# Expert weights in two-way float32r halves, or in raw float32 for groups of 64 and 32 slots: a mixture-of-experts stage on one core

## The chip, the core and the metric

One NeuronCore of a Trainium2 chip runs the whole kernel, one launch for one sequence. The metric is device time in microseconds (us), lower is better. The engines are TensorE (PE), VectorE (DVE), ScalarE (ACT), GpSimd (POOL) and SyncE (SP); SP's queue issues the weight loads.

## The reference

A decoder trunk of two layers on x, 1 x 256 x 1024, all in float32. Each layer has a token mixer and then a channel mixer; both are scaled and shifted by a conditioning vector, and added to x through a gate vector. Layer 0's channel mixer is one dense SwiGLU, layer 1's is this:

```python
logits = h @ router_w                                   # 256 tokens x 8 experts
top_v, top_i = lax.top_k(logits, 2)
gates = jnp.sum(one_hot(top_i, 8) * softmax(top_v)[..., None], axis=-2)
y = jnp.zeros_like(h)
for e in range(8):
    y = y + gates[..., e:e + 1] * ((silu(h @ w1[e]) * (h @ w3[e])) @ w2[e])
x = x + gt_f * y                                        # and a last RMSNorm
```

Here w1 and w3 are 1024 x 2816 and w2 is 2816 x 1024 for each expert. Of all weights, only those of the experts are 277 MB. Each token goes to two of the eight experts.

## The kernel before, in words

The kernel computes both layers up to the router as a *front* that lasts to about 476 us, and then the *expert stage*, which the function `experts` (L761) writes.

**Places.** The experts stand in eight *places*: expert 0 in place 0, the others in places 1 to 7 in descending order of how many tokens chose them (`place`, L861). Each place has a fixed number of *slots* (token rows): 128 in the three *wide* places 0 to 2, 64 in the four places 3 to 6, 32 in place 7 (`slots`, L921). A token past the last slot is taken up by a second pass at the end (L1233 on) that runs only if a flag says so.

**Weights.** Every place streams 33 pieces of 1 MiB (128 x 2048 float32): eleven each of w1, w3 and w2. `load` (L132) issues one DMA on SP's queue, in program order, into the next free tile that `slot` (L122) hands out: in the expert stage first a list `once` (L776: 3 tiles of pool `ahead`, 4 of `more`, 6 of `rawp`, then tiles named `xn` and `big`), and after that `more` and `rawp` in turn, 10 tiles (L779). The 264 loads are all of this form; SP takes them in order, and a load whose tile is not free holds those behind it.

**A wide place.** `prepare` (L928) gathers the place's tokens by matmuls with one-hot matrices (L973), and leaves them as a high and a low float32r part, `x_hi` and `x_lo`. `inner` (L1056) makes six *chunks* of the hidden layer, five of 512 columns and one of 256. Each weight piece is split by `split` (L137) into two halves of 1024 columns, each again a high part (ACT, L145) and a low part (DVE, L146), and `mm3` (L156) issues three float32r matmuls for each product, high by high, high by low and low by high (L157 to L159), on the full 128 x 128 array:

```python
pe.matmul(ps, l_hi, r_hi, ...)      # L157
pe.matmul(ps, l_hi, r_lo, ...)      # L158
pe.matmul(ps, l_lo, r_hi, ...)      # L159
```

`turn` (L996) transposes the chunk. `outer` (L1094) multiplies by w2 in eleven *units*, one weight piece each, again through `split` and `mm3`. `scatter` adds the result to the tokens' rows by matmuls with one-hot matrices.

**A narrow place** (3 to 7). No weight is split. `inner_narrow` (L1029) keeps the tokens in float32, `x_n`, and puts the 64 slots of w1's product into columns 0 to 63 of the array and those of w3's into columns 64 to 127; with 32 slots, each of those halves is halved again for even and odd k:

```python
r = H * i + m * (k % js)            # L1049: m slots, js = 64 // m
pe.matmul(ps[r:r + m, :n], x_n[:, k, :], w[:, kk * n:(kk + 1) * n], ...)
```

`outer` does the same with w2's two column halves (L1099), and `scatter` uses the two halves of the array's rows (L1155).

In the trace a float32 matmul stands as two rows with the form `128*64` (64 columns of the array) or `128*32`; a float32r one is one row, `128*128`.

**Order of the work.** Two streams run in turn: places 0 to 2 and places 3 to 7, each nine steps a place (six chunks, then the outer units in three steps of four, four and three). `TURNS` (L41) is a string of 0 and 1 that says which stream gives the next step. The tile framework sets each engine's queue by priorities within that. The PSUM banks: two of `pb` (wide outer results), two of `pm` (gathers, transposes, scatter), three of `pa` (inner chunks) and one of `po` (narrow outer results).

Of the kernel before, what the change touches and what calls it, by code (L numbers as in the profile page):

```python
# [8 lines left out]
F32 = mybir.dt.float32  # L9
# [19 lines left out]
MORE = 4  # L29
AHEAD = 3  # L30
# [7 lines left out]
HOLD_E = (0, 2, 1, 1, 1)  # L38
WIDE = 3
Q = 32  # L40
# [21 lines left out]
def trunk(  # L62
# [698 lines left out]
    def experts():  # L761
# [70 lines left out]
        def turned(oh, dt):  # L832

            tp = pm()
            tv = tp[:, :SEQ].rearrange("p (t s) -> p t s", t=NT)
            for t in range(NT):
                transpose(tv[:, t, :], oh[:, t, :].bitcast(F32))
            o = et([P, NT, P], "oht", dt, bufs=4)
            act.activation(o[:], tv, AF.Copy)
            return o  # L840

# [6 lines left out]
        pool.memset(cap[:, :WIDE], float(P))  # L848
        pool.memset(cap[:, WIDE:NE - 1], float(H))
        pool.memset(cap[:, NE - 1:], float(Q))  # L850
# [70 lines left out]
        def slots(p):  # L921
            return P if wide_place(p) else H if p < NE - 1 else Q

        def gate_of(p, t):
            return (gates[:, t, 0:1] if p == 0 else placed["gates"][t][:, p:p + 1])

        xe = {}
        def prepare(places):  # L928


            oh = et([P, NT, 2, P], "oh", F32R)
            at = {}
            for i, p in enumerate(places):
                n = slots(p)
                lo_ = i * P + (0 if i else P - n)
                at[p] = lo_, lo_ + n
                for t in range(NT):
                    slot_of = pos[:, t, 0:1] if p == 0 else placed["pos"][t][:, p:p + 1]
                    if wide_place(p):
                        ohi = dve.tensor_scalar(oh[:, t, i, :], iota[:], slot_of, None, op0=ALU.is_equal)  # L940
                    else:
                        ohi = dve.tensor_scalar(oh[:, t, i, :].rearrange("p (i s) -> p i s", s=n),
                                                iota[:, :n].unsqueeze(1).to_broadcast([P, P // n, n]), slot_of, None,
                                                op0=ALU.is_equal)
            base, end = at[places[0]][0], at[places[-1]][1]
            n = end - base
            marks = []
# [13 lines left out]
            xs_of = {}  # L961
            for p in places:
                if wide_place(p):
                    xs_of[p] = et([P, KD, P], "x_hi", F32R), et([P, KD, P], "x_lo", F32R)
                else:
                    xs_of[p] = et([P, KD, slots(p)], "x_n", bufs=2), None
            for k in range(0, KD, 2):
                gp = pm()
                gv = gp[:, :2 * n].rearrange("p (k s) -> p k s", k=2)
                for kk in range(2):  # L970
                    for i, src in enumerate((t_hi, t_lo)):
                        for t in range(NT):
                            pe.matmul(gv[:, kk, :], src[:, t, (k + kk) * P:(k + kk + 1) * P],  # L973
                                      oh[:, t].rearrange("p i s -> p (i s)")[:, base:end],
                                      start=(i + t == 0), stop=(i + t == NT))
                for p in places:
                    r = slice(at[p][0] - base, at[p][1] - base)
                    x_hi, x_lo = xs_of[p]
                    dst = et([P, 2, P], "h32", bufs=2)[:] if wide_place(p) else x_hi[:, k:k + 2, :]
                    for kk in range(2):  # L980
                        ai = act.activation(dst[:, kk, :], gv[:, kk, r], AF.Identity,
                                            bias=B[:, k + kk:k + kk + 1], scale=A[:, k + kk:k + kk + 1])
                    if not wide_place(p):
                        continue
                    dve.tensor_copy(x_hi[:, k:k + 2, :], dst)
                    di = dve.tensor_tensor(x_lo[:, k:k + 2, :], dst, x_hi[:, k:k + 2, :].bitcast(F32),  # L986
                                           op=ALU.subtract)
                    marks.append((ai, di))
            if places[0] == 0:
                hold((HOLD_E[0],), (HOLD_E[1], expd, ohi), *((n_, *m) for n_, m in zip(HOLD_E[2:], marks)))  # L990
            for i, p in enumerate(places):
                xe[p] = (*xs_of[p], turned(oh[:, :, i, :], F32R))

        aa = {}

        def turn(p, c, a):  # L996
# [3 lines left out]
            tp = pm()  # L1000
            tv = tp[:].rearrange("p (b s) -> p b s", b=4)
            for b in range(n):
                ti = transpose(tv[:, b, :], a[:, b * P:(b + 1) * P])
            o = slice(4 * c, 4 * c + n)
            if not aa:

                first.close()
                ap_ = ctx.enter_context(tc.tile_pool(name="inner", bufs=1, side="right", reuse_waits="tile"))
                aa["pool"] = ap_
            if c == 0 and wide_place(p):  # L1010
                for h in ("a_hi", "a_lo"):
                    aa[h] = aa["pool"].tile([P, KF, P], F32R, tag=h, name=nm(h))
            if not wide_place(p):
                m = slots(p)
# [382 lines left out]
```

## Time and profile before

| what | value |
|---|---|
| time, median of 3 runs | 1168.54 us (1166.7 to 1168.91) |
| the profiled execution's own time | 1168.7 us |
| span of its trace, first to last instruction | 1166.9 us |
| PE busy | 1107.4 us, 95% |
| DVE busy | 627.4 us, 54% |
| ACT busy | 518.3 us, 44% |
| moved by DMA | 395.69 MB, mean 339 GB/s |
| mean granted clock of TensorE | 0.979 |

The times of the runs are of the whole execution; the span is of the one profiled execution, and the rows and lines that are read from the trace count from its start. The trace lies 1.8 us below that execution's own time. An engine's busy share is an average over front and expert stage, which have different limits, so each stage has to be read by itself. A row that says `x8` merges eight instructions; its length is from the first one's start to the last one's end.

### The profile page before, as it was taken

To read this page: it belongs to the slowest core of one execution; us is meant where nothing else is said; L and a number is where in the kernel's file an instruction comes from. 1 tells how busy PE (TensorE), PEld (TensorE's weight loads), DVE (VectorE), ACT (ScalarE), POOL (GpSimd) and SP (SyncE) were. 2 spreads that over 40 slices of the span, in tenths; PEclk is the share of its full clock that TensorE was granted. 3 is DMA by queue.
4 is the path that set the end of the run, shared out by engine and by line. 5 is a ranking of instruction groups with operands and counts; after the bars stand their busy time and mean duration, and the time that the engine had idled before them with its cause. 6 is when DMAs were issued, how large, how long until landed. Compare 5 with 4: busy or idle time off the path is not lost.

```text
span 1166.9 us, 15801 instructions
## 1 busy us (share of the span) xinstructions
PE 1107.4 (95%) x6125; PEld 742.8 (64%) x6125; DVE 627.4 (54%) x818; ACT 518.3 (44%) x724; POOL 30.5 (3%) x69
## 2 busy tenths in 40 slices
PE   4899999999999999899999999999999999998993
PEld 2578779999777888686465445554455544655540
DVE  2668556757776765797135443353343633345442
ACT  2764444444437744786234333542342333434331
POOL 2000000000001000300000000000000000000000
PEclk9899999999999999899999999999999999998996
DMA  9977486858886447495999999999999999999994
GB/s 361 410 288 291 145 324 249 310 201 306 334 332 229 147 143 288 181 359 189 418 420 419 420 419 420 419 420 420 388 406 419 420 419 419 419 419 403 398 420 172
DMA packets 57182, 395.69 MB, mean 339 GB/s; under 512 B 8294, under 2 KB 8710, under 8 KB 9356
## 3 DMA queue, kind: packets, MB, share of 16 engines
q1 hardware_dynamic: 54272, 393.24, 84.2%
q10 hardware_dynamic: 2828, 1.37, 0.4%
q8 instruction: 50, 0.82, 0.3%
q14 instruction: 32, 0.26, 0.1%
HBM read 393.53 MB, written 1.05 MB: 338 GB/s over the span
## 4 chain that ended last, share of the span: by engine, by line
PE 88%; DMA 4%; ACT 3%; DVE 2%; POOL 1%; issue 1%; ACTq 0%; POOLq 0%; DVEq 0%; SPq 0%
PE pa L1050 17%; PE pa L158 8%; PE pa L157 8%; PE pa L159 8%; PE po L1099 7%; PE pa L406 6%; PE pa L407 6%; PE pa L408 6%; PE pb L158 4%; PE pb L159 4%; PE pb L157 4%; PE pm L226 2%; PE pb L261 2%; PE pm L973 2%; DMA bdx<-in_wx_dram 2%; ACT whi L145 2%
## 5 line engine op out<-in xcount | busy, mean ns | idle before, releaser
L146 DVE TENSOR_TENSOR wlo<-raw,whi 128x1024 fp32r<-128x1024 f32 x318 | 378.6, 1222 | 205.1 <-ACT whi L145 204.4
L145 ACT ACTIVATE whi<-raw 128x1024 fp32r<-128x1024 f32 x318 | 324.5, 1057 | 214.7 <-PE pa L407 90.2
L1050 PE MATMUL pa<-raw,x_n 128*64 128x512 f32 (+3 forms) x960 | 205.0, 562 | 0.0
L406 PE MATMUL pa<-wide_hi,whi 128*128 128x256 f32 x544 | 154.3, 284 | 0.2 <-DVE wide_hi L380 0.2
L407 PE MATMUL pa<-wide_lo,whi 128*128 128x256 f32 x544 | 153.5, 282 | 0.2 <-DVE wide_lo L381 0.2
L408 PE MATMUL pa<-wide_hi,wlo 128*128 128x256 f32 x544 | 153.5, 282 | 0.0
L1050 PEld LDWEIGHTS pa<-raw,x_n 128*64 128x64 f32 (+1 forms) x960 | 63.0, 131 | 106.7 <-issue 101.3
L158 PE MATMUL pa<-wlo,x_hi 128*128 128x512 f32 (+1 forms) x288 | 113.3, 394 | 3.7 <-DVE wlo L146 3.7
L157 PE MATMUL pa<-whi,x_hi 128*128 128x512 f32 (+1 forms) x288 | 110.7, 389 | 0.9 <-ACT whi L145 0.3
L159 PE MATMUL pa<-whi,x_lo 128*128 128x512 f32 (+1 forms) x288 | 109.9, 382 | 0.1
L406 PEld LDWEIGHTS pa<-wide_hi,whi 128*128 128x128 f32 x544 | 102.3, 188 | 6.4 <-issue 4.0
L407 PEld LDWEIGHTS pa<-wide_lo,whi 128*128 128x128 f32 x544 | 102.5, 189 | 1.6 <-issue 1.1
L408 PEld LDWEIGHTS pa<-wide_hi,wlo 128*128 128x128 f32 x544 | 102.5, 188 | 0.3 <-issue 0.3
L1099 PE MATMUL po<-raw,big 128*64 128x512 f32 (+1 forms) x440 | 93.4, 616 | 6.3 <-DMA raw<-in_m_dram 6.3
L1053 ACT ACTIVATE s<-pa 128x512 f32<-128x512 f32 (+1 forms) x30 | 16.9, 562 | 163.4 <-PE pa L1050 163.4
L158 PE MATMUL pb<-wlo,a_hi 128*128 128x512 f32 x176 | 71.6, 408 | 2.0 <-DVE wlo L146 2.0
L158 PEld LDWEIGHTS pa<-wlo,x_hi 128*128 128x128 f32 x288 | 55.3, 192 | 26.5 <-DVE wlo L146 6.7
L159 PE MATMUL pb<-whi,a_lo 128*128 128x512 f32 x176 | 69.8, 398 | 0.0
L157 PEld LDWEIGHTS pa<-whi,x_hi 128*128 128x128 f32 x288 | 55.3, 192 | 21.8 <-issue 7.7
L157 PE MATMUL pb<-whi,a_hi 128*128 128x512 f32 x176 | 60.8, 403 | 2.0 <-ACT whi L145 2.0
L1099 PEld LDWEIGHTS po<-raw,big 128*64 128x64 f32 (+1 forms) x440 | 25.4, 132 | 57.8 <-issue 49.8
L159 PEld LDWEIGHTS pa<-whi,x_lo 128*128 128x128 f32 x288 | 55.5, 193 | 10.0 <-DVE x_lo L986 0.8
(323 smaller groups left out, 1242.4 us busy)
## 6 DMA issues: line engine op xcount, KB each, us to landing
raw<-in_m_dram SPq DMA_DIRECT2D x263, 1024.0 KB, 10.6
raw<-in_ada_w_dram SPq DMA_DIRECT2D x48, 1024.0 KB, 7.3
raw<-in_f_dram SPq DMA_DIRECT2D x33, 1024.0 KB, 6.0
raw<-in_win_dram SPq DMA_DIRECT2D x20, 1024.0 KB, 6.3
raw<-in_wout_dram SPq DMA_DIRECT2D x8, 1024.0 KB, 6.1
xs<-in_x_dram SPq DMA_DIRECT2D x1, 1024.0 KB
big<-in_m_dram SPq DMA_DIRECT2D x1, 1024.0 KB
out_dram<-big SPq DMA_DIRECT2D x2, 512.0 KB, 3.2
```

The lines of the kernel that those rows point to most:

```text
L145: act.activation(hi[:, :n], src, AF.Copy)
L146: dve.tensor_tensor(lo[:, :n], src, hi[:, :n].bitcast(F32), op=ALU.subtract)
L157: pe.matmul(ps, l_hi, r_hi, start=first, stop=False)
L158: pe.matmul(ps, l_hi, r_lo, start=False, stop=False)
L159: return pe.matmul(ps, l_lo, r_hi, start=False, stop=last)
L226: return pe.transpose(o, i, ident[:i.shape[0], :i.shape[0]])
L261: pe.matmul(ps[o:o + 32, :], cact[:, k, :], wi[:, h * 512:(h + 1) * 512], start=(j == 0), stop=(j == 3))
L406: pe.matmul(pv[:, b, :], wh, h_hi[:, k, :], start=(k == 0), stop=False)
L407: pe.matmul(pv[:, b, :], wh, h_lo[:, k, :], start=False, stop=False)
L408: pe.matmul(pv[:, b, :], wl, h_hi[:, k, :], start=False, stop=(k == KD - 1))
L1050: pe.matmul(ps[r:r + m, :n], x_n[:, k, :], w[:, kk * n:(kk + 1) * n], start=(k < js), stop=(k >= KD - js))
L1099: pe.matmul(acc[r:r + m, :], aa["a_n"][:, k, :], w[:, i * 1024 + c * 512:i * 1024 + (c + 1) * 512], start=(k < js), stop=(k >= KF - js))
```

## The change

No weight of an expert is split any more. Each place is cut into *groups* of 64 or 32 slots (`GROUPS`): places 0 and 2 become 64 + 32 slots, place 1 becomes 64 + 64, places 3 to 7 keep one group. So places 0 and 2 have 96 slots in place of 128. `inner` and `outer` run every group of a place over the same raw float32 weight piece, in the form that the narrow places had. Tokens of wide places stay in float32 (`x_w`), the hidden layer too (`a_w`); the pool of split tiles now ends with the front, and `more` has 10 tiles in place of 4, `ahead` 2 in place of 3. Each group has its own bank and its own one-hot matrix for the scatter, made in a new function `spread` after the eighth unit. The second pass becomes a function that steps through the tokens past the slots 128 at a time.

```diff
-MORE = 4
-AHEAD = 3
+MORE = 10
+AHEAD = 2
...
+GROUPS = ((64, 32), (64, 64), (64, 32), (64,), (64,), (64,), (64,), (32,))
+SLOTS = tuple(sum(g) for g in GROUPS)
...
-    splp = ctx.enter_context(tc.tile_pool(name="splp", bufs=SPLIT_BUFS))
     front = ctx.enter_context(ExitStack())
+    splp = front.enter_context(tc.tile_pool(name="splp", bufs=SPLIT_BUFS))
...
             for p in places:
-                if wide_place(p):
-                    xs_of[p] = et([P, KD, P], "x_hi", F32R), et([P, KD, P], "x_lo", F32R)
-                else:
-                    xs_of[p] = et([P, KD, slots(p)], "x_n", bufs=2), None
+                xe[p] = (et([P, KD, SLOTS[p]], "x_w") if wide_place(p) else et([P, KD, SLOTS[p]], "x_n", bufs=2))
...
+        def groups(p):
+            lo = 0
+            for m in GROUPS[p]:
+                yield lo, m, H // m
+                lo += m
...
+        def spread(p):
+            aa["oht", p] = []
+            for lo, m, _ in groups(p):
+                oh = et([P, NT, P], "oh", F32R)
+                for t in range(NT):
+                    one_hot(oh[:, t, :].rearrange("p (i s) -> p i s", s=m), p, t, lo, m)
+                aa["oht", p].append(turned(oh, F32R))
...
-        def inner(e, c):
-            if not wide_place(e):
-                return inner_narrow(e, c)
...
-                            hi, lo = split(w[:, j * 1024:(j + 1) * 1024])
-                            for kk in range(2):
-                                k = 4 * h + 2 * j + kk
-                                mm3(ps[:], x_hi[:, k, :], x_lo[:, k, :], hi[:, kk * 512:(kk + 1) * 512],
-                                    lo[:, kk * 512:(kk + 1) * 512], k == 0, k == KD - 1)
...
+        def inner(p, c):
+            pss = [pa() for _ in GROUPS[p]]
             n = 512 if c < 5 else 256
             nk = 4 if c < 5 else KD
             for h in range(KD // nk):
+                ws = [load(of_place(w_, p, 2 * c + h)) for w_ in (m1, m3)]
+                for kk in range(0, nk, 2):
+                    for (lo, m, js), ps in zip(groups(p), pss):
+                        for k1 in (kk, kk + 1):
+                            k = nk * h + k1
+                            for i, w in enumerate(ws):
+                                r = H * i + m * (k % js)
+                                pe.matmul(ps[r:r + m, :n], xe[p][:, k, lo:lo + m], w[:, k1 * n:(k1 + 1) * n],
+                                          start=(k < js), stop=(k >= KD - js))
...
+            for ps in pss:
+                a = wk.tile([P, 512], F32, tag="sw" if wide_place(p) else "sn", name=nm("s"))
+                act.activation(a[:, :n], ps[:, :n], AF.Copy)
...
+        def outer(p, units, accs):
+            accs = accs or ([pb() for _ in GROUPS[p]] if wide_place(p)
+                            else [banks[1].tile([P, 512], F32, tag="o", name=nm("po"))])
+            for u in units:
+                w = load(of_place(m2, p, u))
+                for (lo, m, js), acc in zip(groups(p), accs):
                     for i in range(2):
                         k = 2 * u + i
                         for c in range(2):
                             r = H * c + m * (k % js)
+                            pe.matmul(acc[r:r + m, :], aa["a", p][:, k, lo:lo + m],
...
             for t in range(NT):
-                sp = [b() for b in ((pa, pa) if t and e == NE - 1 else (pm, pm))]
-                for i, o in enumerate((o_hi, o_lo)):
+                sp = [b() for b in ((pa, pa) if t and p == NE - 1 else (pm, pm))]
+                for i, (oht, o) in enumerate(parts):
...
+                    if u == 7:
+                        spread(p)
```

PE's queue, in the first inner chunk of place 0 (`x_hi`, `x_lo` or `x_w` the tokens, `raw` a weight piece, `whi` and `wlo` its parts, `pa` the chunk's bank; the shape is that of the result). Before:

```order
L159 MATMUL pa_4509<-whi_4557,x_lo_4447 128x512
L157 MATMUL pa_4509<-whi_4567,x_hi_4446 128x512
L158 MATMUL pa_4509<-wlo_4568,x_hi_4446 128x512
L157 MATMUL pa_4510<-whi_4579,x_hi_4446 128x512
L159 MATMUL pa_4509<-whi_4567,x_lo_4447 128x512
```

After, where `pa_4613` is the bank of the 64-slot group and `pa_4614` that of the 32-slot group:

```order
L1036 MATMUL pa_4614<-raw_4635,x_w_4452 32x512
L1036 MATMUL pa_4614<-raw_4637,x_w_4452 32x512
L1036 MATMUL pa_4613<-raw_4637,x_w_4452 64x512
L1036 MATMUL pa_4613<-raw_4635,x_w_4452 64x512
L1036 MATMUL pa_4613<-raw_4637,x_w_4452 64x512
L1036 MATMUL pa_4614<-raw_4635,x_w_4452 32x512
L1036 MATMUL pa_4614<-raw_4637,x_w_4452 32x512
```

One full-array matmul for each part of each weight gives way to float32 matmuls whose form goes back and forth between 64 and 32 columns of the array within a chunk.

SP's queue where the expert stage's loads begin (`waits` names the engine or the transfer that a load waits for). Before:

```order
L134 DMA raw_4776<-in_m_dram 128x2048 [waits DMAHW7_49,DVE_49]
L134 DMA raw_4577<-in_m_dram 128x2048 [waits PE_49]
L134 DMA raw_4604<-in_m_dram 128x2048 [waits PE_49,Pool_49]
L134 DMA raw_4626<-in_m_dram 128x2048 [waits DMAHW0_49]
L134 DMA raw_4648<-in_m_dram 128x2048 [waits DMAHW1_49]
L134 DMA raw_4906<-in_m_dram 128x2048 [waits DMAHW2_49,DVE_49]
L134 DMA raw_4511<-in_m_dram 128x2048 [waits DMAHW3_49,PE_49]
L134 DMA raw_4533<-in_m_dram 128x2048 [waits DMAHW4_49]
L134 DMA raw_4555<-in_m_dram 128x2048 [waits DMAHW5_49]
```

After:

```order
L135 DMA raw_4831<-in_m_dram 128x2048 [waits DMAHW7_49,DVE_49]
L135 DMA raw_4833<-in_m_dram 128x2048 [waits DMAHW0_49,DVE_49]
L135 DMA raw_4499<-in_m_dram 128x2048 [waits DVE_49]
L135 DMA raw_4501<-in_m_dram 128x2048 [waits PE_49]
L135 DMA raw_4519<-in_m_dram 128x2048 [waits DMAHW1_49,Pool_49]
L135 DMA raw_4521<-in_m_dram 128x2048 [waits DMAHW2_49,PE_49,Pool_49]
L135 DMA raw_4545<-in_m_dram 128x2048 [waits DMAHW3_49]
L135 DMA raw_4547<-in_m_dram 128x2048 [waits DMAHW4_49]
L135 DMA raw_4565<-in_m_dram 128x2048 [waits DMAHW5_49]
```

The load whose tile lies where the mixer's last multiply on DVE still reads (`gate_m`, L440; the row that waits for `DVE_49` alone, raw_4499) stands third in the rows of after, ahead of those into the tiles that come free earlier; before, the one that stands in that room (raw_4906) is behind four others.

## Rows read from the trace of the kernel before

**Rows 1.** Windows of the expert stage, by engine; last columns granted clock, DMA share, GB/s

```profile
core 0: us, PE busy (x) PEld busy (x) DVE busy (x) ACT busy (x) POOL busy (x), PEclk, DMA share, GB/s
476.00:543.00 67.00, 65.82 (x305) 53.41 (x307) 57.14 (x81) 53.77 (x78) 8.83 (x17) 0.94 0.65 241
543.00:625.00 82.00, 82.00 (x417) 47.61 (x413) 32.02 (x44) 30.83 (x46) 0.00 (x0) 1.00 0.94 386
625.00:1065.00 440.00, 432.78 (x1971) 228.47 (x1971) 187.80 (x209) 157.55 (x221) 0.00 (x0) 1.00 1.01 416
1065.00:1151.00 86.00, 72.63 (x412) 36.28 (x411) 34.78 (x43) 29.27 (x42) 0.00 (x0) 0.95 0.94 388
```

**Rows 2.** Page, costliest groups: out<-in, shapes, xcount | busy us, mean ns | idle before

```profile
L1050 PE MATMUL pa<-raw,x_n 128*64 128x512 f32 (+3 forms) x960 | 205.0, 562 | 0.0
L1099 PE MATMUL po<-raw,big 128*64 128x512 f32 (+1 forms) x440 | 93.4, 616 | 6.3 <-DMA raw<-in_m_dram 6.3
L146 DVE TENSOR_TENSOR wlo<-raw,whi 128x1024 fp32r<-128x1024 f32 x318 | 378.6, 1222 | 205.1 <-ACT whi L145 204.4
```

**Rows 3.** Timeline of PE: start us, length us, line, form, xcount; 64-wide runs

```profile
570.94 7.09 PE L1050 MATMUL pa<-raw,x_n 128*64 128x512 f32 x32
577.96 0.44 PE L226 MATMUL pm<-ident,s 128*128 128x128 f32 x2
...
709.94 3.65 PE L1050 MATMUL pa<-raw,x_n 128*64 128x512 f32 x14
713.52 0.66 PE L226 MATMUL pm<-ident,s 128*128 128x128 f32 x4
```

**Rows 4.** Timeline of PE, a chunk of a split expert, first and last of 33

```profile
699.76 0.39 PE L158 MATMUL pa<-wlo,x_hi 128*128 128x512 f32 x1
...
707.25 0.39 PE L157 MATMUL pa<-whi,x_hi 128*128 128x512 f32 x1
```

**Rows 5.** Timeline of PE, gathers, a 64-wide run of eight rows, gathers

```profile
745.49 0.39 PE L973 MATMUL pm<-oh,t_hi 128*128 128x128 f32 x2
745.72 0.39 PE L973 MATMUL pm<-oh,t_lo 128*128 128x128 f32 x2
746.03 1.94 PE L1099 MATMUL po<-raw,big 128*64 128x512 f32 x8
747.90 0.44 PE L973 MATMUL pm<-oh,t_hi 128*128 128x128 f32 x2
```

**Rows 6.** Timeline of PE, one 32-wide matmul, then a full-array one

```profile
1103.63 1.04 PE L1050 MATMUL pa<-raw,x_n 128*32 128x512 f32 x2
1104.61 0.50 PE L158 MATMUL pb<-wlo,a_hi 128*128 128x512 f32 x1
```

**Rows 7.** Lines' first and last start (us), two timeline rows of DVE and PE

```profile
L973 PE MATMUL pm<-oh,t_hi x96: 222/276/476, 476.3 to 1006.1; 128*128 128x128 f32 x80, 128*128 128x32 f32 x16
L1099 PE MATMUL po<-raw,big x440: 589/592/1063, 625.0 to 1150.0; 128*64 128x512 f32 x118, 128*32 128x512 f32 x29
L157 PE MATMUL pa<-whi,x_hi x208: 276/395/503, 564.6 to 1065.2; 128*128 128x512 f32 x80, 128*128 128x256 f32 x24
467.53 0.69 DVE L440 TENSOR_TENSOR y<-pa,gate_m 128x512 f32<-128x512 f32 x1 [1.80 <-PE pa L159]
1154.01 0.63 PE L1155 MATMUL pa<-ob,oht 64*128 64x512 f32 x2
```

**Rows 8.** Waits of PE, 476 to 1152: total us, times, longest

```profile
PE po L1099 <- DMA raw<-in_m_dram: 6.3, 5, 1.5
PE pm L226 <- ACT s L1053: 5.2, 9, 0.7
```

**Rows 9.** Timeline of PE, scatter, then a 64-wide run

```profile
798.07 0.50 PE L1155 MATMUL pm<-ob,oht 64*128 64x512 f32 x2
798.50 3.65 PE L1050 MATMUL pa<-raw,x_n 128*64 128x512 f32 x16
```

**Rows 10.** Timeline of PE, last unit of the last expert

```profile
1149.16 1.94 PE L1099 MATMUL po<-raw,big 128*32 128x512 f32 x8 [0.64 <-DMA raw<-in_m_dram]
```

More of the change, by code (lines that the diff above doesn't have):

```diff
@@ L847, in experts @@
         pool.tensor_copy(idx[:], idx_i[:])
[L848 to L850 removed]
+        for p in range(NE):
+            pool.memset(cap[:, p:p + 1], float(SLOTS[p]))
         sq = [P, NE, NE]
@@ L999, in turn @@
+        def turn(p, c, parts):
             n = 4 if c < 5 else 2
[L1000 to L1003, printed above, removed]
             o = slice(4 * c, 4 * c + n)
-            if not aa:
+            if "pool" not in aa:
                 first.close()
-                ap_ = ctx.enter_context(tc.tile_pool(name="inner", bufs=1, side="right", reuse_waits="tile"))
-                aa["pool"] = ap_
@@ new lines, in turn @@
+            for (lo, m, js), a in zip(groups(p), parts):
+                dst = aa["a", p][:, o, lo:lo + m]
+                tp = pm()
+                tv = tp[:].rearrange("p (b s) -> p b s", b=4)
+                for b in range(n):
+                    ti = transpose(tv[:, b, :], a[:, b * P:(b + 1) * P])
+                g = wk.tile([P, 4, m], F32, tag="s", name=nm("g"))
+                if js == 1:
+                    ai = act.activation(g[:, :n, :], tv[:, :n, :H], AF.Silu)
+                    di = dve.tensor_tensor(dst, g[:, :n, :], tv[:, :n, H:], op=ALU.mult)
+                else:
+                    both = wk.tile([P, 4, 2, m], F32, tag="s", name=nm("q"))
+                    tq = tv.rearrange("p b (i j s) -> p b i j s", i=2, j=2)
+                    act.activation(both[:, :n], tq[:, :n, :, 0, :], AF.Copy)
+                    dve.tensor_tensor(both[:, :n], both[:, :n], tq[:, :n, :, 1, :], op=ALU.add)
+                    ai = act.activation(g[:, :n, :], both[:, :n, 0, :], AF.Silu)
+                    di = dve.tensor_tensor(dst, g[:, :n, :], both[:, :n, 1, :], op=ALU.mult)
+                late[:] = ti, ai, di
@@ L1087, in outer @@
-        def outer(e, units, acc):
-            if not wide_place(e):
-                m = slots(e)
-                js = H // m
-                acc = acc or banks[1].tile([P, 512], F32, tag="o", name=nm("po"))
-                for u in units:
-                    w = load(of_place(m2, e, u))
+                ws = [load(of_place(w_, p, 2 * c + h)) for w_ in (m1, m3)]
[7 more added lines that the diff above has]
+                                          start=(k < js), stop=(k >= KD - js))
@@ L1181, in rest_of @@
                         place_rest()
-                        gate_halves(aa["last"])
+                        gate_halves(late[1])
                         prepare((WIDE, WIDE + 1))
@@ L1229, in experts @@
         with ExitStack() as order:
-            for i in (*aa["late"], last_load[0]):
+            for i in (*late, last_load[0]):
                 order.enter_context(tc.issue_after(i.ins))
@@ L1293, in experts @@
+                for begin in range(0, (SEQ if e < WIDE else 2 * SEQ // e) - SLOTS[e], P):
+                    with tc.If(mine > 0):
+                        past_slots(e, begin)
             last_norm()
```

295 lines of the change are left out of this document (96 added, 199 removed).

## The prediction

> **What bounds the kernel now.** I read the windows of the expert stage first, then the page's costliest groups, then PE's timeline for the price of each form, and last PE's waits. The windows [rows 1] show PE busy for 432.8 of 440 us between 625 and 1065, with DMA at its full share, 416 GB/s; that is 2.52 us for a piece of 1 MiB. Both limits stand at once there. Neither ACT nor DVE is near its own: DVE is busy 188 of those 440 us. The two outer windows show slack on the DMA side (0.65 at the start) and on PE's (72.6 of 86 at the end). The groups [rows 2] show where PE's time goes beside the split matmuls, and what a split costs off PE: 1.22 us on DVE for each. PE's waits [rows 8] are small: 6.3 us for weights in five waits, 5.2 us for ACT's evictions in nine. So a change in this stage is worth what it takes from PE *and* from the stream; one alone gives nothing there. What a gain on PE could at most uncover is the stream.
>
> **Prices on PE.** Every price comes from the timeline.
> - A run of 32 rows of the 64-wide form is 16 matmuls, two at a time in the two column halves of the array [rows 3]. With the 0.16 us that the way out of the form takes (below) left off, 7.02 us are 8 pairs of 0.857; I take 0.855 us per pair, 0.43 for one matmul. The run of 14 rows is 7 matmuls and took 3.58 us from its start to the next form's: 4 times 0.855 and 0.16. An odd half is paid whole.
> - The 32-wide form goes four at a time: 0.21 each. One alone took 0.98 us until the next form began [rows 6], which is 0.855 and 0.125.
> - A full-array float32r matmul of 512 columns: 32 steps in 7.49 us [rows 4], 0.234; of 256 columns 0.117. A 128 x 128 gather or transpose: 0.23 for two [rows 5], 0.11 each.
> - A change of form between full array and column halves: eight rows (4 matmuls, two pairs, 1.71 us) began 0.09 us late and left 0.16 us late [rows 5], so 0.125 a change in the mean. Between a scatter (row halves) and the column halves 0.43 us stand for a pair of about 0.23 [rows 9], so 0.2.
>
> **PE's work, by the code's loops.** Before: each wide place has 372 full-array steps of 512 columns and 48 of 256; with scatter 1140 and 144. So 1140 x 0.234 + 144 x 0.117 + 384 gathers and transposes x 0.11 = 325.8 us. Narrow places: 560 64-wide matmuls (64 of them of 256 columns), 225.7; 140 32-wide ones, 28.2; 40 scatter halves, 4.7. Sum 584.5. By the order of PE's queue, odd halves add 22.9, and 188 changes of form 23.5: 630.9. The trace has 678.3 between the first gather at 476.3 and the last scatter's end at 1154.6 [rows 7]. The other 47 are 6.6 at the start (first narrow outer step at 625.0, where the work up to there is 142.1; the granted clock is 0.94 until 543 [rows 1]), 18 in the middle, where the stream paces PE, and 22.7 at the end, where PE waits for the last loads [rows 10].
>
> After: the 1116 + 144 split steps are gone, and with them 198 splits, 198 x 1.222 = 242 us of DVE and a like part of ACT. They lie off the path, under PE's work; nothing is gained by them directly. The three wide places become 560 more 64-wide matmuls and 280 more 32-wide ones: in all 1120 (128 of 256 columns), 451.5; 420 (48), 84.7; 456 gathers and transposes, 50.2; 88 scatter halves, 10.3. Sum 596.7: **12 us more PE work**, though 64 slots fewer are computed. Odd halves rise to 46.9, since the two groups of places 0 and 2 cut the runs short: 643.6. Changes of form rise to 313, of which 129 are between two column forms, nearly all 64-wide to 32-wide and back.
>
> **The unknown price.** No row of before shows a change from the 64-wide to the 32-wide form. Its bounds: nothing (both forms use one kind of tile, and no weights are on the other half), even a gain if halves of different forms overlap; and 0.2 us by the scatter's row [rows 9]. I take 0.125, the mean in and out of the column forms [rows 5, 6], since the pipeline there empties in the same way, and count odd halves as paid at these changes too. With that, 313 x 0.125 = 39.1 and PE's work is 682.7. At 0.06 it is 674, at 0.2 it is 692; with nothing, and overlap, 661. The Trainium skill, "TensorEngine Tiling (Array Packing)", section "Tiling Modes", says that a change of the tiling mode, not of the tile alone, drains the engine; the trace agrees where rows exist (0.09 and 0.16 us around eight rows), and no run here shows it between the two column forms. By that rule all 129 cost like the others and the work is 682.7; without it 661.
>
> **The stream.** 264 loads of 2.52 us are 665 us. Before, SP's rows have four pieces into tiles that come free earlier ahead of the one that waits for DVE's last use of that room; after, six pieces have their tiles early, and the seventh waits in SP's queue behind the mixer's last multiply, which ends at 468.2 [rows 7], with all the others behind it, as SP's rows show. The other 258 take 650 us: the stream could end at 1118, some 35 us before PE with its new work. Once PE is the bound, the stream waits for tiles (16 pieces, 40 us ahead), its share falls below one, and the 22.7 us wait at the end shrinks; I leave 5 us for the last loads, about four waits at 1.3 [rows 8]. Ten more tiles thus buy no time by themselves: a queue that is ahead of its consumer.
>
> **The rest.** The wide chunk's eviction now is a copy on ACT per group and its own transposes through two `pm` banks, where before there was one; it is hidden behind the other stream's matmuls as the narrow ones were (5.2 us of waits [rows 8]). The new memsets on POOL and the one-hots of `spread` run beside PE. The front is untouched. The second pass is behind a flag that stays zero.
>
> **The sum.** 476.3 + 6.6 + 682.7 + 5 = 1170.6 for the last scatter's end, against 1154.6: +16.0. The norm and the store behind it keep their 12.3 us. The profiled execution took 1168.7 in all, 0.2 over the median, so the sum is put on the median: 1168.5 + 16 = **1184 us**. Given price bounds of 0.06 to 0.2 and evictions that bite a little, this case spans 1171 to 1200.
>
> **Rivals.**
> *The column forms mix freely* (the price is zero and halves overlap, no barrier). Then PE's work is 661, and more waits for the last loads come up, 8.6 us: 476.3 + 6.6 + 661 + 8.6 = 1152.5, 2 us below before: 1166, between 1160 and 1171. For it: a 64-wide matmul already starts on one half while the other still works [rows 3]. Against: every change that the trace shows costs something. Chance 0.22, of which 0.12 over 0.2% faster, 0.08 within, 0.02 slower.
> *The other side, faster: the stream becomes the bound.* If also odd halves are filled across every boundary, PE needs 596.7 and 184 changes to or from the full array, 23: 619.7. The point is a PE work of about 635 (1118 less 476.3 less 6.6): below it the stream's end at 1118 decides, and from the last unit's start to the span's end are 17.7 us [rows 10]: a span of 1136, 1138 with what lies around it, to 1147 with stalls for tiles; I take 1141. For it: SP's deeper queue, and a stage that no split paces. Against: the odd run of seven, which paid its whole half [rows 3]. Chance 0.12.
> *New waits.* Two groups share two `pm` banks and one ACT chain. 66 group chunks at 5.2/9 = 0.58 us [rows 8] are 38 us at the most: 1200 to 1222. Chance 0.08. Against: before, narrow chunks did the same in their turns.
> That the change does not do what it says is part of the sum: the larger room does not start the stream earlier.
>
> **How the numbers follow.** A measurement of this kernel can tell about 0.2%, 2.3 us. The forecast has 0.58, all of it slower. Faster: 0.12 + 0.12 = 0.24; same 0.08; slower 0.58 + 0.02 + 0.08 = 0.68. The range 1160 to 1200 holds the forecast and the first rival and leaves out the other two, 0.20.
>
> **What would show it.** Right: between 625 and 1065 PE stays busy at its share while DMA falls to about 0.93 and SP's loads wait for PE; in the timeline, at a change from 64 to 32 columns, the next run starts some 0.1 us late; the first narrow outer step comes at 628 to 634 in place of 625.0; the splits' rows are gone from DVE and ACT. Wrong: runs of both forms that overlap, or wide runs whose time is below 0.855 a pair; DMA at its full share to the end, which is the second rival; PE waits for ACT at the transposes in most chunks, which is the third.

## The result and the profile after

The change is slower: 1197.36 us (median of 4 runs, 1196.92 to 1198.51) against 1168.64 for the kernel before in the same comparison. The ratio is 1.0251, with a 95% interval of 1.0233 to 1.0269. The forecast was 1184, its range 1160 to 1200: the sign and the place were right, and the loss is 28.7 us where 16 were forecast.

From the page of the changed kernel (the span, busy times, and three of the costliest groups):

```profile
span 1195.2 us, 16333 instructions
PE 1148.1 (96%) x6641; PEld 623.3 (52%) x6641; DVE 392.1 (33%) x630; ACT 346.5 (29%) x577; POOL 28.0 (2%) x74
...
L1036 PE MATMUL pa<-raw,x_w 128*64 128x512 f32 (+3 forms) x1136 | 242.1, 568 | 0.0
...
L147 DVE TENSOR_TENSOR wlo<-raw,whi 128x1024 fp32r<-128x1024 f32 x122 | 148.6, 1221 | 74.2 <-ACT whi L146 73.8
...
L1056 PE MATMUL po<-raw,big 128*64 128x512 f32 (+1 forms) x440 | 93.6, 597 | 2.2 <-DMA raw<-in_m_dram 2.2
```

DVE lost 235 us of work and ACT 172, as the splits went (122 of them are left, all in the front, where [rows 2] had 318), and none of that is in the time. PE gained 41 us. The windows of the expert stage, in the columns of [rows 1]:

```profile
476.00:543.00 67.00, 66.56 (x348) 24.59 (x350) 8.10 (x33) 15.65 (x40) 5.74 (x17) 0.94 0.93 379
543.00:625.00 82.00, 82.00 (x478) 30.93 (x474) 6.70 (x19) 14.90 (x37) 0.00 (x0) 1.00 0.93 376
625.00:1065.00 440.00, 436.88 (x2095) 158.28 (x2092) 43.85 (x96) 53.88 (x124) 0.00 (x0) 1.00 0.95 381
1065.00:1151.00 86.00, 83.03 (x507) 24.50 (x509) 11.38 (x29) 12.65 (x30) 0.00 (x0) 1.00 0.98 404
```

Between 625 and 1065 the stream fell from 416 GB/s [rows 1] to 381, and PE is busy throughout. At the start the stream is much faster than before (379 against 241 GB/s), which is the larger room at work (with the tiles of before it is 210, run 3), and PE takes no more from it. The waits of PE from 476 on (total us, times, longest), to compare with [rows 8]:

```profile
PE pm L227 <- ACT s L1041: 6.8, 10, 0.7
PE po L1056 <- DMA raw<-in_m_dram: 2.2, 2, 1.5
PE pm L1077 <- ACT ob L1068: 1.5, 1, 1.5
PE pm L961 <- DVE oh L926: 0.6, 1, 0.6
```

So PE is the bound from the first gather to the last units. The other side of the same wait is SP's queue (same columns; `SPq` is the queue that issues the loads), which waits for PE to give tiles back:

```profile
SPq L135 <- PE pa L1036: 370.3, 113, 11.9
```

What PE's time consists of shows in two pieces of its timeline, each with the row behind it (start, length, line, form, rows):

```profile
1085.48 7.76 PE L1036 MATMUL pa<-raw,x_w 128*64 128x512 f32 x32
1093.06 1.02 PE L1036 MATMUL pa<-raw,x_n 128*32 128x512 f32 x2
...
1112.99 11.52 PE L1056 MATMUL pb<-raw,a_w 128*64 128x512 f32 x64
1124.33 3.62 PE L1036 MATMUL pa<-raw,x_n 128*32 128x512 f32 x32
```

**The price of a change between column forms.** The third row is four outer units of a wide place, 64 rows of both forms (the row prints the form of its first). Each unit is four 64-wide matmuls and then four 32-wide ones: 8 pairs and 4 fours, 12 steps of 0.857 us, 10.29. It took 11.34 until the next row, which begins in the form that it ended in, so there are 7 changes inside and 1.05 us over: **0.15 us a change**, above the 0.125 that the forecast took and below its upper bound.

**The odd halves.** The first row is half an inner chunk: 16 matmuls, 4 pairs and 2 fours, 5.14 us. It took 7.58. PE's queue has these rows here (raw_7386 is w1's piece, raw_7388 w3's; the first eight of sixteen, the other eight are four and four):

```
L1036 MATMUL pa_7364<-raw_7386,x_w_6346 64x512
L1036 MATMUL pa_7365<-raw_7386,x_w_6346 32x512
L1036 MATMUL pa_7364<-raw_7388,x_w_6346 64x512
L1036 MATMUL pa_7364<-raw_7386,x_w_6346 64x512
L1036 MATMUL pa_7364<-raw_7388,x_w_6346 64x512
L1036 MATMUL pa_7365<-raw_7388,x_w_6346 32x512
L1036 MATMUL pa_7365<-raw_7386,x_w_6346 32x512
L1036 MATMUL pa_7365<-raw_7388,x_w_6346 32x512
```

One matmul on w1 goes alone in either form, before w3's first. Six runs make five changes, 0.75 us. The other 1.69 are two steps of 0.857: one and three 64-wide matmuls are three steps where four are two, one and three 32-wide ones are two steps where four are one. In those steps part of the array stands empty.

### The profile page after: what moved, and what is told of

Read it like the earlier page. It is cut to its first block, busy times and chain, and to the rows that moved or that the text cites. A ratio compares the mean times of both kernels' runs of the same rounds, so it can differ in the third digit from the quotient of the medians.

```text
span 1195.2 us, 16333 instructions
## 1 busy us (share of the span) xinstructions
PE 1148.1 (96%) x6641; PEld 623.3 (52%) x6641; DVE 392.1 (33%) x630; ACT 346.5 (29%) x577; POOL 28.0 (2%) x74
## 3 DMA queue, kind: packets, MB, share of 16 engines
HBM read 393.53 MB, written 1.05 MB: 330 GB/s over the span
## 4 chain that ended last, share of the span: by engine, by line
PE 92%; DMA 4%; ACT 1%; DVE 1%; issue 0%; POOL 0%; ACTq 0%; POOLq 0%; SPq 0%
PE pa L1036 35%; PE pb L1056 9%; PE po L1056 7%; PE pa L407 6%; PE pa L409 5%; PE pa L408 5%; PE pm L227 4%; PE pa L158 3%; PE pa L159 3%; PE pa L160 3%; PE pm L961 2%; PE pb L262 2%; DMA raw<-in_m_dram 2%; PE pb L160 1%; PE pb L158 1%; PE pb L159 1%
## 5 line engine op out<-in xcount | busy, mean ns | idle before, releaser
L1036 PE MATMUL pa<-raw,x_w 128*64 128x512 f32 (+3 forms) x1136 | 242.1, 568 | 0.0
L147 DVE TENSOR_TENSOR wlo<-raw,whi 128x1024 fp32r<-128x1024 f32 x122 | 148.6, 1221 | 74.2 <-ACT whi L146 73.8
L146 ACT ACTIVATE whi<-raw 128x1024 fp32r<-128x1024 f32 x122 | 128.4, 1059 | 147.4 <-PE pa L408 88.1
L1036 PEld LDWEIGHTS pa<-raw,x_w 128*64 128x64 f32 (+1 forms) x1136 | 71.0, 127 | 148.1 <-issue 141.8
L1041 ACT ACTIVATE s<-pa 128x512 f32<-128x512 f32 (+1 forms) x66 | 37.1, 562 | 350.1 <-PE pa L1036 321.0
L1056 PE MATMUL pb<-raw,a_w 128*64 128x512 f32 (+1 forms) x528 | 104.9, 601 | 0.0
L1056 PEld LDWEIGHTS pb<-raw,a_w 128*64 128x64 f32 (+1 forms) x528 | 27.3, 127 | 68.2 <-issue 67.1
L267 DVE SCALAR_TENSOR_TENSOR acc<-raw,cs,acc 128x1024 f32<-128x1024 f32 x37 | 47.4, 1281 | 12.5 <-DMA raw<-in_ada_w_dram 8.7
L227 PEld LDWEIGHTS pm<-ident,s 128*128 128x128 f32 x242 | 25.5, 141 | 46.7 <-issue 23.2
L262 PE MATMUL pb<-raw,cact 128*32 128x512 f32 x224 | 31.5, 647 | 16.3 <-DMA raw<-in_ada_w_dram 16.3
```

Of the source, the lines that this page charges most:

```text
L146: act.activation(hi[:, :n], src, AF.Copy)
L147: dve.tensor_tensor(lo[:, :n], src, hi[:, :n].bitcast(F32), op=ALU.subtract)
L227: return pe.transpose(o, i, ident[:i.shape[0], :i.shape[0]])
L262: pe.matmul(ps[o:o + 32, :], cact[:, k, :], wi[:, h * 512:(h + 1) * 512], start=(j == 0), stop=(j == 3))
L1036: pe.matmul(ps[r:r + m, :n], xe[p][:, k, lo:lo + m], w[:, k1 * n:(k1 + 1) * n], start=(k < js), stop=(k >= KD - js))
L1056: pe.matmul(acc[r:r + m, :], aa["a", p][:, k, lo:lo + m], w[:, i * 1024 + c * 512:i * 1024 + (c + 1) * 512], start=(k < js), stop=(k >= KF ...
```

## The experiments

Unless another baseline is named, differences are against the change's 1197.36 us; ratios are to the kernel before, run beside each.

**1. Pairs.** An edge for the scheduler: in each k of an inner chunk the matmul on w1 goes behind the one on w3, so that it is never issued alone.

```diff
-                            for i, w in enumerate(ws):
-                                r = H * i + m * (k % js)
-                                pe.matmul(ps[r:r + m, :n], xe[p][:, k, lo:lo + m], w[:, k1 * n:(k1 + 1) * n],
-                                          start=(k < js), stop=(k >= KD - js))
+                            with ExitStack() as order:
+                                for i in (1, 0):
+                                    r = H * i + m * (k % js)
+                                    mi = pe.matmul(ps[r:r + m, :n], xe[p][:, k, lo:lo + m],
+                                                   ws[i][:, k1 * n:(k1 + 1) * n],
+                                                   start=(k < js), stop=(k >= KD - js))
+                                    if i:
+                                        order.enter_context(tc.issue_after(mi.ins))
```

> The change, with one ordering added in the inner chunks: for each k the matmul on w1 is queued behind the one on w3, so that the two column halves of a 64-wide (or 32-wide) product always stand next to each other in PE's queue. Theory P (PE's queue sets the time, and its odd halves and changes of form are what the change added): by the queue's order the odd halves fall from 44 to 7 us and the changes of form from 313 to 289, at 0.16 us each 4 us, so some 40 us less PE work: 1150 to 1165 us against 1197.4, unless waits for w3 take part of it. Theory S (the stream's tiles and its late start set the time): within 5 us of 1197. Theory E (evictions on ACT and the transposes behind them set it): within 5 us of 1197, with PE's waits for L1041 as they were or longer.

Measured: 1171.54 us, 25.8 less than the change; ratio 1.0038 (1.0023 to 1.0053). One edge gives back nearly all that the change lost. PE's timeline of this run has the same half chunk without an odd half:

```profile
1061.80 5.80 PE L1037 MATMUL pa<-raw,x_w 128*64 128x512 f32 x32
1067.41 1.90 PE L1037 MATMUL pa<-raw,x_n 128*32 128x512 f32 x16
```

5.61 us to the next row in place of 7.58: 5.14 and three changes. Theories S and E fall. The direction is theory P's, but the time lies above its 1150 to 1165. PE's busy time from 476 on fell by 35.0 us (696.0 to 661.0), and 9 of that came back as waits: they are 20.0 us where the change has 11.1, most of them for copies and scatters on ACT and DVE, 3.1 for loads. In the windows of this run (columns of [rows 1]) PE has gaps and DMA is back near its full share, and the last three units of the last expert wait for their loads (the last of them below), so that the end hangs on the stream:

```profile
625.00:1065.00 440.00, 429.81 (x2188) 152.15 (x2188) 49.70 (x107) 55.54 (x129) 0.00 (x0) 1.00 0.98 401
1065.00:1151.00 86.00, 79.96 (x584) 24.42 (x580) 12.28 (x30) 14.35 (x34) 0.00 (x0) 0.98 1.00 410
```

```profile
1140.55 7.07 PE L1060 MATMUL po<-raw,big 128*32 128x512 f32 x64
...
1152.81 1.06 PE L1060 MATMUL po<-raw,big 128*32 128x512 f32 x8 [1.51 <-DMA raw<-in_m_dram]
```

**2. Turned loops.** In the inner chunk all 64-slot matmuls of a pair of pieces come first, and in the outer step the units are loaded together and each group runs over them.

```diff
-                for kk in range(0, nk, 2):
+                for kk in range(0, nk, nk):
...
-            for u in units:
-                w = load(of_place(m2, p, u))
-                for (lo, m, js), acc in zip(groups(p), accs):
+            ws = [load(of_place(m2, p, u)) for u in units]
+            for (lo, m, js), acc in zip(groups(p), accs):
+                for u, w in zip(units, ws):
```

> The change, with the loops turned round: in a chunk all 64-slot matmuls of a pair of pieces come before all 32-slot ones, and in the outer step all units of a step are loaded first and each group then runs over them. Theory P: 44 changes of form fewer (313 to 269), at 0.16 us 7 us, odd halves unchanged (44.6): 1188 to 1193 us. Theory C (the changes from 64 to 32 columns alone are the loss, at a price nearer 0.3 with their odd halves): 48 of 129 gone, 15 us or more: 1182 or below. Theory S: a little slower, since pieces are held longer: 1197 to 1205.

Measured: 1193.73 us, 3.6 less and 0.7 above theory P's range; ratio 1.0228. By the time, 44 changes fewer are worth 0.08 us each. PE's busy time from 476 on fell by 5.3 us (696.0 to 690.7), 0.12 a change, and 1.3 of that came back as waits for the last loads (3.5 us in place of 2.2). Theory C (0.3 a change) falls.

**3. The stream's tiles as before.**

```diff
-MORE = 10
-AHEAD = 2
+MORE = 4
+AHEAD = 3
```

> The change, with the stream's tiles as before: MORE 4 and AHEAD 3 in place of 10 and 2. Theory P: the ten tiles buy next to nothing, since PE is the bound: 1192 to 1200 us (6 changes of form and 2 us of odd halves fewer by the queue's order), with more waits of SP for PE. Theory S (the deeper stream is what holds the time at 1197, or its late start is what costs): over 1205, or under 1190.

Measured: 1212.18 us, 14.8 *more*; ratio 1.0382. Theory P's number was wrong, and the time lies where theory S put it (over 1205): the tiles are worth 15 us, though run 1 shows that they are not what sets the time of the change. Where they are worth it, the timeline of the last expert's outer units shows. First the change, then this run:

```profile
1166.42 1.04 PE L1056 MATMUL po<-raw,big 128*32 128x512 f32 x8
...
1167.98 7.07 PE L1056 MATMUL po<-raw,big 128*32 128x512 f32 x64
1175.76 1.06 PE L1056 MATMUL po<-raw,big 128*32 128x512 f32 x8 [0.70 <-DMA raw<-in_m_dram]
1178.33 1.06 PE L1056 MATMUL po<-raw,big 128*32 128x512 f32 x8 [1.50 <-DMA raw<-in_m_dram]
```

```profile
1167.28 1.06 PE L1056 MATMUL po<-raw,big 128*32 128x512 f32 x8 [0.57 <-DMA raw<-in_m_dram]
...
1182.26 1.06 PE L1056 MATMUL po<-raw,big 128*32 128x512 f32 x8 [0.86 <-DMA raw<-in_m_dram]
1184.75 1.93 PE L1056 MATMUL po<-raw,big 128*32 128x512 f32 x8 [1.43 <-DMA raw<-in_m_dram]
...
1192.31 1.06 PE L1056 MATMUL po<-raw,big 128*32 128x512 f32 x8 [0.81 <-DMA raw<-in_m_dram]
```

With 16 tiles in turn, eight units run one behind the other in 7.07 us, and two wait. With 10 tiles all of the last eleven wait, and start 2.5 us apart, the length of a piece on the stream. While PE is the bound, the stream can be ahead by as many pieces as there are tiles; the last expert costs PE 0.86 us a unit, so the end uses the head start up. Six pieces of 2.52 us are 15.1; from the first of these units to the last are 11.91 us in the change and 25.03 here, so 13.1 of the 14.8 us arise there.

**4. Both, pairs and turned loops** (the edits of 1 and 2).

> Both of the above, pairs and turned loops. Theory P: odd halves 10 us, 244 changes of form: 45 us less PE work than the change: 1145 to 1162 us, below the kernel before. Theory S: no better than 1195.

Measured: 1171.85 us; ratio 1.0038 (1.0024 to 1.0052), the same as pairs alone, and above the 1145 to 1162 of theory P. 45 changes of form fewer are worth nothing here, because the end hangs on the loads. The last expert's units that run one behind the other start 2.4 us before those of run 1 (1140.55), and the last unit starts when run 1's does (1152.81):

```profile
1138.14 6.21 PE L1060 MATMUL po<-raw,big 128*32 128x512 f32 x56
...
1152.77 1.72 PE L1060 MATMUL po<-raw,big 128*32 128x512 f32 x8 [0.64 <-DMA raw<-in_m_dram]
```

**5. Seven tiles in `more`** (`MORE = 7` in place of 10, `AHEAD` 2 as in the change).

> The change with MORE 7 in place of 10: 13 tiles in the stream's turn, not 16. Theory L (the tiles are a head start that is used up at the end, where the last expert's units leave PE faster than pieces arrive: each tile is one piece, 2.5 us): 3 tiles of the 6 that the run with MORE 4 lacked, so half of its 14.8 us: 1203 to 1206 us, all of it behind 1151 as PE's waits for the last loads. Rival F (in the run with MORE 4 the late first loads and AHEAD 3 made the difference): within 2 us of 1197. PE's work is the same within 1 us by the queue's order.

Measured: 1207.84 us, 10.5 more and 1.8 above theory L's range; ratio 1.0337. The rival falls. The last expert's first and last outer units in this run:

```profile
1169.19 1.04 PE L1056 MATMUL po<-raw,big 128*32 128x512 f32 x8
...
1187.46 1.93 PE L1056 MATMUL po<-raw,big 128*32 128x512 f32 x8 [0.64 <-DMA raw<-in_m_dram]
```

From the first to the last are 18.27 us, against 11.91 in the change and 25.03 in run 3. So three tiles fewer cost 6.4 us there and six cost 13.1: 2.1 to 2.2 a tile, somewhat less than a piece of 2.52. Theory L's dose is right in kind, but not all of the 10.5 us lies where it said. The first of these units already starts 2.8 us later than in the change, though the first narrow outer unit starts at the same time (632.5 and 632.6), and some 2 us more lie behind the last unit. Where the 2.8 us arise stays open.

**6. Two groups of 64 in places 0 and 2.**

```diff
-GROUPS = ((64, 32), (64, 64), (64, 32), (64,), (64,), (64,), (64,), (32,))
+GROUPS = ((64, 64), (64, 64), (64, 64), (64,), (64,), (64,), (64,), (32,))
```

> The change with places 0 and 2 as two groups of 64 slots too, so that hardly a change between 64 and 32 columns is left (5 of 129). By the queue's order 56.6 us more products, 20 us fewer odd halves, 114 changes of form fewer: at 0.16 us each PE's work grows by 18.5, to 1214 to 1218 us. Rival C (a change between the two column forms costs 0.3 us or more): under 1202. Rival N (these changes cost nothing): 1232 or more.

Measured: 1212.27 us, 14.9 more and 1.7 below the range; ratio 1.0383. Both rivals fall. Solved for the price by the time: 56.6 - 20 - 14.9 = 21.7 us for 114 changes, 0.19 each. But PE also waits less here (6.0 us in place of 11.1), so the time shows too little of the work. PE's busy time from 476 on grew by 19.1 us (696.0 to 715.1), and 56.6 - 20 - 19.1 = 17.5 us are 0.15 each, the price in the timeline. The 32-slot groups earn their place, though not by much: 57 us of products saved, some 38 paid in changes and odd halves.

**7. Pairs, the 32-slot place first, and mixed turns.**

```diff
+NARROW = (7, 3, 4, 5, 6)
-TURNS = "00000" + "110" * 18 + "10" * 4 + "11111"
+TURNS = "000" + "110" * 20 + "10" * 4 + "1"
...
-        streams = [all_steps(range(WIDE)), all_steps(range(WIDE, NE))]
+        streams = [all_steps(range(WIDE)), all_steps(NARROW)]
```

> The pairs of the first run, and the steps in another order: the 32-slot place first among the narrow ones, and the turns 000, then 110 twenty times, 10 four times, 1, in place of 00000, 110 eighteen times, 10 four times, 11111. So pieces that cost PE 0.86 us stand beside the wide pieces at the start, and wide steps go on to the end. Theory B (in the run with pairs, PE and the stream are both near their bounds, and the stream lost time early, where PE held its tiles, and PE lost it late, where it waited for the last loads): PE's work is 650 us as there, the waits at the end and the last expert's transposes go: 1155 to 1163 us against 1171.5. Rival: the order of the steps is worth nothing, 1168 to 1174.

Measured: 1180.38 us, 8.8 more than pairs alone; ratio 1.0110. A miss. SP's queue starts the experts' loads at 467.76, where the change starts them at 421.75 (timeline of SP's queue, this run and then the change):

```profile
467.76 10.18 SPq L136 DMA_DIRECT2D raw<-in_m_dram  x11
```

```profile
421.75 56.83 SPq L135 DMA_DIRECT2D raw<-in_m_dram  x17
```

The six tiles that come free first stand last in the list of first tiles. As long as they hold pieces of place 0, the scheduler takes these loads ahead. With 000 they fall to place 7, whose expert is known only after the router, and the six pieces come late, 15 us of stream. PE, which was busy for 88.75 of these 89 us in run 1, pays between 543 and 632:

```profile
543.00:632.00 89.00, 78.63 (x544) 25.74 (x542) 11.49 (x30) 15.71 (x39) 0.00 (x0) 0.96 1.01 419
```

**8. The same with the inner loops of 2.**

> The run before, and in the inner chunks all 64-slot products of a pair of pieces ahead of the 32-slot ones: 35 changes of form fewer. At 0.16 us each, 5 us faster than the run before if PE's queue is the bound: 1150 to 1158; as fast as that one if the stream is.

Measured: 1176.68 us, 3.7 less than run 7, and with it far above the 1150 to 1158 expected; ratio 1.0072. 35 changes fewer at 0.11 each: here PE is the bound again at the end (busy for 84.55 of 86 us between 1065 and 1151, with DMA at 0.82).

**9. Early pieces to early tiles.** Run 8 with the turns of the change, and the first pieces into `rawp`:

```diff
-        once.extend([ahead] * AHEAD + [more] * MORE + [rawp] * RAW_BUFS)
+        once.extend([rawp] * RAW_BUFS + [ahead] * AHEAD + [more] * MORE)
...
-        pools[:] = [more] * MORE + [rawp] * RAW_BUFS
+        pools[:] = [rawp] * RAW_BUFS + [more] * MORE
```

> Pairs and 64-slot rows ahead of 32-slot rows as in the last run, the 32-slot place first among the narrow ones, but the first run's turns again (00000 first), and the first six pieces go to the six tiles that come free earliest (rawp ahead of the others in the list). Theory B (the two runs before this one lost 16 us between 543 and 632, because their first loads started at 468 and not at 421, and gained behind it): the six early pieces are back, PE's work is 649 us by the queue's order: 1155 to 1164 us, below the kernel before. Rival (the new order of the places is itself what cost them): 1172 or more, with waits of PE for weights.

Measured: 1168.45 us; ratio 1.0005 (0.9996 to 1.0014), as fast as the kernel before, 29 us below the change, and 4 above what was expected. The loads start at 422.25 again, and PE is busy for 87.5 of 89 us between 543 and 632, as it should be if the late loads cost run 7 that time. But the turns went back too, and how much of the 8.2 us to run 8 each of the two gives was not separated. The stream is at its full share from 632 to 1065 and then runs out, while PE works on:

```profile
1000.00:1065.00 65.00, 61.75 (x342) 21.04 (x340) 8.23 (x18) 8.11 (x19) 0.00 (x0) 0.95 1.01 419
1065.00:1151.00 86.00, 83.28 (x438) 26.86 (x434) 8.51 (x18) 7.78 (x16) 0.00 (x0) 1.00 0.76 315
```

That unsplit weights in groups come out even with split ones here is no comparison of like with like, since the kernel before still has its odd halves. With the same edge in both, the split weights are 6 us ahead: 1165.30 (run 10) against 1171.54 (run 1).

**10. The kernel before, with pairs.** The edge of run 1 in `inner_narrow`; nothing of the change.

> The kernel before with only the pairs in its narrow inner chunks. By the queue's order its PE work falls by 28 us (odd halves 22 to 2 us, 188 changes of form to 144). Theory B (before, the stream paces PE from 625 on, so that PE's work is no longer what sets the time): 1160 to 1168 us, a gain of at most 8. Rival (PE's queue sets the time of both kernels): 1140 to 1146.

Measured: 1165.30 us; ratio 0.9977 (0.9967 to 0.9987), 2.8 less than before. The same edge that is worth 26 us in the change is worth 3 here, though by the queue's count it takes 28 us from PE's work; PE's busy time from 476 on fell by 22 (655.4 to 633.6). The window shows why (columns of [rows 1]; first the kernel before, then this run):

```profile
632.00:1065.00 433.00, 425.78 (x1942) 225.92 (x1939) 187.80 (x209) 157.55 (x221) 0.00 (x0) 1.00 1.01 416
632.00:1065.00 433.00, 412.34 (x1993) 227.30 (x1989) 195.09 (x218) 166.22 (x233) 0.00 (x0) 1.00 1.01 419
```

13 us less PE work, and the stream was at its full share already.

**11. That, with the 32-slot place first** (`NARROW` as in run 7).

> The kernel before with pairs, and the 32-slot place first among the narrow ones, the turns as they were. Theory B (split weights; the stream sets the time and loses it early, where PE holds its tiles: share 0.62 until 543 and 0.93 until 632): light narrow pieces beside place 0 let PE free tiles sooner, so that the share between 543 and 632 comes to 1.0: 1158 to 1163 us. Rival (the last narrow place with 64 slots makes the end longer than that): 1165 or more.

Measured: 1163.88 us; ratio 0.9965 (0.9951 to 0.9978). Just above Theory B's range, and not by its mechanism: the share between 543 and 632 stays at 0.94, and the gain on run 10 is 1.4 us, which the intervals of the two ratios don't tell from none.

```profile
543.00:632.00 89.00, 75.33 (x482) 42.76 (x479) 32.99 (x49) 31.07 (x52) 0.00 (x0) 0.95 0.94 387
```

**12. That, with the mixed turns of run 7.**

> The same, with the first narrow step after three wide ones in place of five (000, 110 twenty times, 10 four times, 1). Theory B: PE frees tiles sooner still, in the stretch where the share was 0.62: 5 to 12 us below the run before it, 1148 to 1158. Rival (the first narrow pieces wait for the places' numbers, as in the run where 000 stood first without early pieces): no better than 1163.

Measured: 1160.57 us; ratio 0.9934 (0.9920 to 0.9948): **faster than both kernels**, by 8 us and by 37. It keeps the split weights and the 10 tiles. Its first two windows, and behind them the second one of the kernel before:

```profile
476.00:543.00 67.00, 65.67 (x319) 46.69 (x320) 47.73 (x73) 46.73 (x70) 8.85 (x17) 0.94 0.67 257
543.00:632.00 89.00, 74.10 (x461) 43.10 (x461) 34.43 (x51) 31.30 (x51) 0.00 (x0) 0.94 1.01 419
543.00:632.00 89.00, 89.00 (x449) 50.17 (x447) 32.02 (x44) 30.83 (x46) 0.00 (x0) 1.00 0.94 389
```

The stream reaches its full share between 543 and 632, where the kernel before has 389 GB/s. That narrow pieces leave PE sooner than split ones is the reason that the expectation gave; no run tests it by itself. The gain on run 11 is 3.3 us of the 5 to 12 expected, and the first window, at 0.67, is hardly better.

## Why the prediction was right, and where its size was off

**The bound: right.** PE's content decides, as the forecast case said: PE is busy for 436.9 of 440 us, DMA's share falls to 0.95 (0.93 was named), SP waits for PE, and the first narrow outer unit starts at 632.6 (628 to 634 was named; [rows 7] have 625.0). The stream starts as forecast, too: six early loads, and the seventh at 468.40. Run 1 is the test: PE's order alone, changed by one edge, moves the time by 26 us.

**The unknown price: right within its bounds, low by a fifth.** "I take 0.125" should have been 0.15, by the timeline of the outer units and by PE's busy time in run 6; the turned loops gave 0.12 (run 2). For the 129 changes between column forms that is some 3 us; if all 313 cost as much, they are 47.0 us and not 39.1, and PE's work is 690.6 and not 682.7. That a change between two column forms has a price like one between a column form and the full array, the trace bears out: 0.15 us here, 0.09 and 0.16 in [rows 5]. The Trainium skill ("TensorEngine Tiling (Array Packing)", section "Tiling Modes") says that a change of the tiling mode drains the engine, and lists 128x64 and 128x32 as separate configurations; the trace agrees, with these 0.15 us.

The trace has as much work. From the first gather at 476.4 to the last scatter's end at 1182.9 are 706.5 us; 11.1 of them are waits, and about 5.4 are the clock's, whose granted share is 0.83 for 24 us at the start and 0.96 for 32 us at the end:

```profile
476.00:500.00 24.00, 23.56 (x106) 9.52 (x108) 5.35 (x25) 4.26 (x11) 5.74 (x17) 0.83 1.01 419
1151.00:1183.00 32.00, 27.53 (x208) 9.17 (x206) 8.56 (x15) 4.43 (x10) 0.00 (x0) 0.96 0.81 334
```

That leaves 690.0, 7.3 more than forecast. How much of the 7.3 is this price, and how much the counts (the expectations of runs 1 and 2 have 44 and 44.6 us of odd halves, not 46.9) and the other prices, was not measured apart.

**Odd halves: right in size, wrong in the reason, and the largest of the terms that the change added.** They were counted as a term, 22.9 and then 46.9 us: 24 more, against 12 of products and 16 to 19 of changes. But the working gave the reason as the two groups' short runs. The reason is the scheduler's order, which sets matmuls on w1 ahead of w3's first ones, so that each lone one leaves half of the array empty. In the kernel before the same order stands in the narrow places and is hidden behind the stream (run 10). A term of 47 us that an order makes, and no product needs, should have been listed as what to undo.

**The waits: low.** "I leave 5 us for the last loads" held for those (2.2 us). The step "The rest" put evictions at nothing, hidden as before; the named waits of PE come to 11.1 us in all, 6.8 of them for the copies on ACT, ten times 0.7 at a chunk's transposes. That is not the third rival's mechanism, two groups of a wide place in each other's way: nine of the ten stand right behind a run of a narrow place, which has one group, like this one, and the kernel before has nine waits for such copies, 5.2 us [rows 8].

```profile
1128.69 0.66 PE L227 MATMUL pm<-ident,s 128*128 128x128 f32 x4 [0.74 <-ACT s L1041]
```

**The tiles: wrong.** "Ten more tiles thus buy no time by themselves" failed. It is six more that stand in turn, 16 in place of 10, and they bought 14.8 us (run 3), most of it by the head start at the end. The text saw that the 22.7 us of waits at the end shrink, and put that shrinking into the sum by leaving 5, but took it for a result of PE's greater work and not of the tiles. With 4 and 3 tiles the change would have come to 1212.

**The rivals.** Neither the free mix (1166) nor the stream as the bound (1141) came about; the second shows itself once the odd halves are gone, at 1171 us, where the end hangs on the loads (runs 1 and 4).

**The sum.** The last scatter's end came at 1182.9, 12.3 us behind the forecast's 1170.6, and the same 12.3 us follow it. PE's work is 7.3 of that, and the waits are 6.1 (11.1 in place of 5); the 5.4 us of the clock stand where the forecast had 6.6 for the start, so that term was about right.

## What to carry to other kernels

Count an engine's work by its queue's order and not by the list of products: forms that share the array in halves are paid in pairs, and one lone matmul costs as much as two. An order of the scheduler is worth an edge where the engine is the bound, and nearly nothing where the stream is; look which it is before writing one. Tiles of a prefetch are a head start: where the last work is lighter than the stream, each is worth up to one piece's transfer at the end (2.1 to 2.2 us here, of 2.52), and little before that.

## What the runs showed that was not expected

A head start can be priced: in the last expert's units six tiles fewer cost 13.1 us and three cost 6.4. That the whole of run 3's loss, 14.8 us, is within 2% of six pieces of 2.52 is partly luck, since run 5's 10.5 us are not near three of them. A change between 64 and 32 columns of the array costs as much as one to the full array, 0.15 us, though only the width of the column groups differs. And one edge on PE's order was worth 26 us where PE is the bound and 3 where the stream is (runs 1 and 10); with it in both, three float32r passes over split weights are 6 us ahead of float32 in column groups.
